# Letting the first scores of the last layer in a few products later

## The chip, the cores and the metric

The kernel runs on one core of a Trainium2 chip, in one launch. The metric is the device time of that launch in microseconds, taken as the median of several runs. TensorE multiplies matrices, VectorE and ScalarE do elementwise work and reductions, GpSimd does a little arithmetic and issues some loads, and SyncE issues most of the loads.

## The reference

Two layers act on 256 latent tokens (`x`) and 256 context tokens (`ctx`) of width 2048. Each layer has one wide input projection whose columns are shared out among three branches: a gated MLP that mixes positions, windowed attention with grouped queries, and a Fourier mix. The branches are gated, joined and projected back. The change touches the attention of the second layer, where only the latent tokens ask:

```
def window_attention(q, k, v, k_ctx, v_ctx, sink):
    ...
    s_loc = jnp.einsum('bnqkgd,bnjkd->bnkgqj', qb, kw).astype(jnp.float32) * scale
    s_ctx = jnp.einsum('bnqkgd,bmkd->bnkgqm', qb, k_ctx).astype(jnp.float32) * scale
    ...
    s_loc = jnp.where(mask[None, :, None, None], s_loc, NEG_INF)
    sk = sink_column(sink, (bsz, nb, B_KV_HEADS, B_GROUP, CHUNK))
    n_ctx = k_ctx.shape[1]
    p = jax.nn.softmax(jnp.concatenate([sk, s_ctx, s_loc], axis=-1), axis=-1)
    p_ctx = p[..., 1:1 + n_ctx].astype(v.dtype)
    p_loc = p[..., 1 + n_ctx:].astype(v.dtype)
    o = (jnp.einsum('bnkgqm,bmkd->bnqkgd', p_ctx, v_ctx)
         + jnp.einsum('bnkgqj,bnjkd->bnqkgd', p_loc, vw))
    return o.reshape(bsz, s, B_WIDTH)
```

There are 8 query heads of width 128 and 2 key/value heads. Queries and keys of the latent tokens are rotated (`rope_2d`) first.

## The kernel before, in words

Every large product is done in split precision. A weight tile `raw` of 128x1024 is loaded, ScalarE rounds it to a high part `whi` (L458) and VectorE subtracts to get the low part `wlo` (L460). Activations are split in the same way into pairs (`split_into`, L507 on ScalarE and L508 on VectorE).

TensorE's instruction order is written out by hand. In layer 1 a unit of 128 projected columns (`tunit1`) is 8 products of 512 columns (L627) on the first weight tile, 8 of 256 columns with its low part (L629), 8 of 256 with the second tile's low part, and 8 of 512 on the second tile. There are 8 such units for the queries (phase `q1`), one per head, and then 8 for the gate of the attention (phase `bg1`). When a unit is done, `joined` adds its two halves (L612 on ScalarE, L613 on VectorE).

The attention of a head is a generator, `attention(h, ps)`, that runs beside the units behind its own. Its pieces are these:

- the rotation of the query (`rope`: four copies L932 on ScalarE, L934 to L936 on VectorE) and its split (L507, L508);
- the scores: six products of 512 columns (L490 to L492) into two tiles `sc`, one per half of the queries; then the mask (L954), the row maximum (L956), the exponentials (L969, L976), the sum (L979), its reciprocal (L980) and the scaling of the probabilities (L985);
- twice, a group of four transposes (L1005) whose result is copied to a split pair (L507 of 512 columns on ScalarE, L508 on VectorE), and behind each such pair six products with the values into `o` (L490 to L492), one step later.

Between the pieces the generator yields a delay. A small clock, `Later`, holds them: each product of a unit moves it on by what the product is reckoned to take (`PASS`), and a piece whose delay has passed is emitted there, in TensorE's order, between two products of a unit. The delays are `YQ` from the rotation to the scores, `YA` from the scores to the first transposes, and `YB` from one group of transposes to the next:

```
    YQ, YA, YB = [5.5, 6.8], [10.0, 8.6], [3.8, 4.0]
```

A delay counts from where the piece before was really emitted. ScalarE's, VectorE's and SyncE's orders are not written by hand in this part: a scheduler sorts their instructions by priority, dependences and its own reckoning of times, and the engines then keep to that order.

Beside all this VectorE multiplies the modulation weights of the last gate, two instructions per loaded tile `mraw` (L290), placed among the other work as its priority allows.

Of the kernel before, what the change touches and what calls it, by code (L numbers as in the profile page):

```python
# [66 lines left out]
def trunk_kernel(ctx: ExitStack, tc: tile.TileContext, xT, xhalf, cT, wss, wsl, wmod, win, wout0, wout1, const, vec, rows,  # L67
# [9 lines left out]
    def sb(shape, dt, tag, bufs=1):  # L77
        cnt[0] += 1
        return pool.tile(shape, dt, tag=tag, bufs=bufs, name=f"{tag}_{cnt[0]}")

    def w2k(shape, dt=F32):
        return sb(shape, dt, "w2k", W2K)

    def mm_ps(name="mm"):
        cnt[0] += 1
        return psum.tile([P, 512], F32, tag="mm", bufs=6, name=f"ps_{name}_{cnt[0]}")

    def ms_ps(name="ms"):
        cnt[0] += 1
        return psum.tile([P, 512], F32, tag="ms", bufs=2, name=f"ps_{name}_{cnt[0]}")  # L90
# [251 lines left out]
    NX, AHEADX, LATE = 4, 2, 12  # L342
    YX, YC, YE = [2.4, 1.4, 1.8], 1.5, 5.0
    YQ, YA, YB = [5.5, 6.8], [10.0, 8.6], [3.8, 4.0]

    def pace():

        state["owed"] += RATE.get(state["phase"], 0.0) / 2
        while state["owed"] >= 1:
            state["owed"] -= 1  # L350
            with low(LAG), tc.issue_after(W.last.ins):
                next(mods, None)
# [136 lines left out]
    def mm3(ps, st, mv, start, stop):  # L489
        PE.matmul(ps, st[0], mv[0], start=start, stop=False)  # L490
        PE.matmul(ps, st[0], mv[1], start=False, stop=False)  # L491
        PE.matmul(ps, st[1], mv[0], start=False, stop=stop)  # L492

    def part(w, c):

        def of(t):
            if not isinstance(t, list):
                return t[:, c]
            n = t[0].shape[-1]
            return t[c.start // n][:, c.start % n:c.start % n + c.stop - c.start]  # L500

        return of(w[0]), of(w[1])
# [3 lines left out]
    def split_into(hi, lo, src):  # L506
        A.copy(hi, src)  # L507
        V.tensor_tensor(out=lo, in0=src, in1=hi.bitcast(F32), op=ALU.subtract)  # L508
        return hi, lo
# [134 lines left out]
    def layer(l):  # L644
        last = l == 1
# [278 lines left out]
        def rope(hi, lo, ps, ctx=None):  # L924

            if ctx is None and hi.shape[-1] > S:
                ctx = ps[:, S:T]
            nrot[0] += 1
            rot = rots[nrot[0] % 4]
            for a in range(4):  # L930
                b = a ^ 1
                A.copy(rot[32 * a:32 * a + 32], ps[32 * b:32 * b + 32, 0:S])  # L932
            t = w2k([P, S])
            V.tensor_tensor(out=t, in0=ps[:, 0:S], in1=cc("cos"), op=ALU.mult)  # L934
            V.tensor_tensor(out=rot, in0=rot, in1=cc("sin"), op=ALU.mult)
            V.tensor_tensor(out=rot, in0=rot, in1=t, op=ALU.add)  # L936
            split_into(hi[:, LAT], lo[:, LAT], rot)
            if hi.shape[-1] > S:
                split_into(hi[:, CTX], lo[:, CTX], ctx)
# [4 lines left out]
        def attention(h, ps):  # L944
            g = h // 4
            q = w2k([P, n], F32R), w2k([P, n], F32R)
            rope(*q, ps)
            yield YQ[l]
            sc, mx = [], sb([P, 4], F32, "mx", 2)
            for b in range(2):  # L950
                s = mm_ps("sc")
                mm3(s, part(q, slice(b * P, (b + 1) * P)), kt[g], True, True)
                edge = s[:, (1 - b) * P:(2 - b) * P]
                V.tensor_tensor(out=edge, in0=edge, in1=split["m0"][:, b], op=ALU.add)  # L954
                sc.append((s, T))
                V.tensor_reduce(out=mx[:, b:b + 1], in_=s, axis=mybir.AxisListType.X, op=ALU.max)  # L956
            if not last:
                s = mm_ps("scc")
                for b in range(2):
                    mm3(s[:, b * S:(b + 1) * S], part(q, slice(S + b * P, S + (b + 1) * P)),  # L960
                        part(kt[g], CTX), True, True)
                sc.append((s, S))
                V.tensor_reduce(out=mx[:, 2:4], in_=s.rearrange("p (b k) -> p b k", k=S),
                                axis=mybir.AxisListType.X, op=ALU.max)
            nm = sb([P, 4], F32, "nm", 2)
            V.tensor_scalar(out=nm[:, :nt], in0=mx[:, :nt], scalar1=-SCALE, scalar2=nskb[:, h:h + 1],
                            op0=ALU.mult, op1=ALU.min)
            es = sb([P, 4], F32, "es", 2)
            A.activation(es[:, :nt], nm[:, :nt], AF.Exp, bias=skb[:, h:h + 1])  # L969
            den = sb([P, 4], F32, "den", 2)  # L970
            prob = []
            for i, (s, w) in enumerate(sc):
                p = w2k([P, T])
                for b in range(T // w):
                    c = i + b
                    A.activation(p[:, b * w:(b + 1) * w], s[:, b * w:(b + 1) * w], AF.Exp, scale=SCALE,  # L976
                                 bias=nm[:, c:c + 1], accum_out=den[:, c:c + 1])
                prob.append(p)
            V.tensor_tensor(out=den[:, :nt], in0=den[:, :nt], in1=es[:, :nt], op=ALU.add)  # L979
            V.reciprocal(den[:, :nt], den[:, :nt])  # L980
            for i, (s, w) in enumerate(sc):
                for b in range(T // w):
                    c = i + b
                    with low(LOWP[l]):
                        A.activation(prob[i][:, b * w:(b + 1) * w], prob[i][:, b * w:(b + 1) * w], AF.Copy,  # L985
                                     scale=den[:, c:c + 1])
            yield YA[l]
            o, pts = None, []

            def pv(half):  # L990
                for j in range(2):
                    kk = 2 * half + j
                    dst, kv = (o[:, LAT], kk) if half < 2 else (o[:, CTX], 2 + j)
                    mm3(dst, part(vv, slice(kv * 256 + g * P, kv * 256 + (g + 1) * P)),
                        part(pts[half], slice(j * S, (j + 1) * S)), kk in (0, 4), kk in (3, 5))

            halves = 2 if last else 3
            for half in range(halves):
                tp = ms_ps("tp")
                for j in range(2):  # L1000
                    for b in range(2):
                        kk = 2 * half + j
                        src = prob[b][:, kk * P:(kk + 1) * P] if half < 2 else \
                            prob[2][:, b * S + j * P:b * S + (j + 1) * P]
                        PE.transpose(tp[:, (2 * j + b) * P:(2 * j + b + 1) * P], src, ident)  # L1005
                pts.append(split_into(w2k([P, 512], F32R), w2k([P, 512], F32R), tp))
                if half == 0:
                    o = mm_ps("o")
                else:
                    pv(half - 1)  # L1010
                yield YB[l]
            pv(halves - 1)
            A.copy(ysl(4 + h), o[:, 0:n])
# [57 lines left out]
        for h in range(8):  # L1071
            ps = tunit1([0])[0] if last else tunit(n)
            later.add(attention(h, ps))
            later.tick(0.0)
# [385 lines left out]
```

## Time and profile before

| what | value |
|---|---|
| median of three runs | 1130.13 us (1129.95 to 1130.45) |
| profiled execution, its time | 1130.9 us |
| profiled execution, its span | 1129.1 us |
| TensorE busy | 1118.5 us, 99% of the span |
| VectorE busy | 928.0 us, 82% |
| ScalarE busy | 526.0 us, 47% |
| mean granted TensorE clock | 0.999 |

The profile is of one execution. Its span runs from the first to the last instruction; the time of the run has 1.8 us more around it. In the timeline, each row has the start in us, the duration, the engine, the line of the kernel, the operation, what it writes and reads, and how many equal instructions were merged; a bracket tells how long the engine had been idle before it and whose work ended that.

### The profile page before, as it was taken

The page shows a single profiled execution, that of the slowest core. Times are in us where ns is not written, and L with a number is a line of the kernel's source. Part 1 is how long each engine was busy: PE and PEld are TensorE (multiplying, and loading weights), DVE is VectorE, ACT ScalarE, POOL GpSimd, SP SyncE. Part 2 cuts the span into 40 slices and gives each one's busy share as a digit, 9 for nine tenths or more (in the row PEclk, how much of TensorE's full clock was granted, in tenths as well). Part 3 has the DMA queues.
Part 4 walks back from the last instruction along what each step waited for, and adds up shares of the span by engine and source line. Part 5 has one row for each costly group of instructions (what it writes and reads, how often), then busy time and mean ns, then how long its engine had stood idle before and what let it go on. Part 6 is the DMA issues. An engine that isn't in the chain of part 4 may idle for free.

```text
span 1129.1 us, 16606 instructions
## 1 busy us (share of the span) xinstructions
PE 1118.5 (99%) x6108; PEld 920.4 (82%) x6108; DVE 928.0 (82%) x1633; ACT 526.0 (47%) x992; POOL 32.9 (3%) x43
## 2 busy tenths in 40 slices
PE   8999999999999999999999999999999999999998
PEld 3666788888888888888888888988888888888886
DVE  1578799989888897888999989396988788878874
ACT  5322533322234667632523334266665369867541
POOL 0000000000000000000000000030500000000000
PEclk9999999999999999999999999999999999999999
DMA  9999655566655344365566665385956785456972
GB/s 364 402 402 400 244 172 187 183 205 200 211 180 187 119 141 130 121 204 174 182 188 221 206 205 185 96 193 191 226 180 205 225 282 177 147 186 196 304 259 75
DMA packets 75138, 235.85 MB, mean 209 GB/s; under 512 B 8608, under 2 KB 13104, under 8 KB 75056
## 3 DMA queue, kind: packets, MB, share of 16 engines
q1 hardware_dynamic: 70272, 229.79, 60.8%
q0 software_dynamic: 4064, 3.69, 2.2%
q10 hardware_dynamic: 720, 1.31, 0.3%
q8 instruction: 48, 0.79, 0.3%
q14 instruction: 34, 0.28, 0.1%
HBM read 232.65 MB, written 2.10 MB: 208 GB/s over the span
## 4 chain that ended last, share of the span: by engine, by line
PE 94%; DMA 3%; ACT 1%; DVE 1%; issue 0%; ACTq 0%; POOLq 0%; DVEq 0%
PE ps_t L490 15%; PE ps_t L491 15%; PE ps_t L492 15%; PE ps_t L627 10%; PE ps_t L629 5%; PE ps_v L1065 3%; PE ps_y L490 3%; PE ps_y L492 3%; PE ps_y L491 3%; PE ps_av L490 2%; PE ps_mod L182 2%; PE ps_av L491 2%; PE ps_av L492 2%; PE ps_tp L1005 2%; PE ps_v L1067 1%; PE ps_au L490 1%
## 5 line engine op out<-in xcount | busy, mean ns | idle before, releaser
L458 ACT CAST whi<-raw 128x1024 fp32r<-128x1024 f32 (+1 forms) x209 | 216.2, 1037 | 292.5 <-PE ps_t L491 217.0
L460 DVE TENSOR_TENSOR wlo<-raw,whi 128x1024 fp32r<-128x1024 f32 (+1 forms) x209 | 251.0, 1205 | 50.4 <-ACT whi L458 43.8
L490 PE MATMUL ps_t<-hh,whi 128*128 128x512 f32 (+1 forms) x752 | 290.7, 387 | 0.0
L491 PE MATMUL ps_t<-hl,whi 128*128 128x512 f32 (+1 forms) x752 | 289.6, 385 | 0.0
L492 PE MATMUL ps_t<-hh,wlo 128*128 128x512 f32 (+1 forms) x752 | 289.4, 385 | 0.0
L252 DVE SCALAR_TENSOR_TENSOR macc<-mraw,cs,macc 128x512 f32<-128x512 f32 x360 | 251.0, 747 | 13.3 <-DMA mraw<-in_wmod_dram 12.8
L492 PEld LDWEIGHTS ps_t<-hh,wlo 128*128 128x128 f32 x752 | 141.3, 188 | 28.7
L490 PEld LDWEIGHTS ps_t<-hh,whi 128*128 128x128 f32 x752 | 141.3, 188 | 26.8
L491 PEld LDWEIGHTS ps_t<-hl,whi 128*128 128x128 f32 x752 | 141.4, 188 | 26.2
L627 PE MATMUL ps_t<-hh,whi 128*128 128x512 f32 x512 | 132.7, 394 | 0.0
L627 PEld LDWEIGHTS ps_t<-hh,whi 128*128 128x128 f32 x512 | 92.6, 188 | 16.8
L629 PE MATMUL ps_t<-hh,wlo 128*128 128x256 f32 x512 | 72.5, 282 | 0.0
L629 PEld LDWEIGHTS ps_t<-hh,wlo 128*128 128x128 f32 x512 | 68.5, 190 | 2.4
L572 ACT ACTIVATE hh<-w2k,sh 128x256 fp32r<-128x256 f32 x48 | 22.0, 502 | 73.5 <-DVE w2k L568 73.5
L490 PE MATMUL ps_y<-whi,hh 128*128 128x512 f32 x104 | 41.3, 397 | 0.0
L492 PE MATMUL ps_y<-whi,hh 128*128 128x512 f32 x104 | 40.6, 390 | 0.0
L491 PE MATMUL ps_y<-wlo,hh 128*128 128x512 f32 x104 | 40.5, 389 | 0.0
L490 PE MATMUL ps_av<-whi,hh 128*128 128x512 f32 x94 | 39.0, 415 | 0.6 <-ACT hh L572 0.6
L491 PE MATMUL ps_av<-wlo,hh 128*128 128x512 f32 x94 | 37.0, 394 | 0.0
L507 ACT CAST w2k<-ps_tp 128x512 fp32r<-128x512 f32 x40 | 23.4, 585 | 20.8 <-PE ps_scc L491 13.7
L508 DVE TENSOR_TENSOR w2k<-ps_tp,w2k 128x512 fp32r<-128x512 f32 x40 | 27.5, 688 | 4.7 <-ACT w2k L507 2.2
L612 ACT COPY join<-ps_t 128x256 f32<-128x256 f32 x34 | 12.4, 370 | 39.0 <-PE ps_t L627 38.9
(460 smaller groups left out, 1736.8 us busy)
## 6 DMA issues: line engine op xcount, KB each, us to landing
raw<-in_win_dram SPq DMA_DIRECT2D x160, 512.0 KB, 4.2
mraw<-in_wmod_dram SPq DMA_DIRECT2D x128, 512.0 KB, 4.3
raw<-in_wout_dram SPq DMA_DIRECT2D x60, 512.0 KB, 4.3
mraw<-in_wsl_dram SPq DMA_DIRECT2D x14, 512.0 KB, 7.1
yo<-in_wsl_dram SPq DMA_DIRECT2D x16, 256.0 KB, 7.2
macc<-in_wsl_dram SPq DMA_DIRECT2D x7, 512.0 KB, 7.7
vv<-in_wsl_dram SPq DMA_DIRECT2D x7, 512.0 KB, 8.3
mg<-in_wsl_dram SPq DMA_DIRECT2D x7, 512.0 KB, 9.0
```

Source lines behind the costliest of these rows:

```text
L182: PE.matmul(self.ps[32 * kk:32 * kk + 32, 0:self.N], cpad[:, kg * 4 + kk], self.w[kg * 4 + kk], start=kg == 0, stop=kg == 3, tile_position ...
L252: V.scalar_tensor_tensor(out=acc[:, s], in0=w[:, kk % 2], scalar=c, in1=acc[:, s], op0=ALU.mult, op1=ALU.add)
L458: A.copy(ph, rc)
L460: self.last = V.tensor_tensor(out=pl, in0=rc, in1=ph.bitcast(F32), op=ALU.subtract)
L490: PE.matmul(ps, st[0], mv[0], start=start, stop=False)
L491: PE.matmul(ps, st[0], mv[1], start=False, stop=False)
L492: PE.matmul(ps, st[1], mv[0], start=False, stop=stop)
L507: A.copy(hi, src)
L508: V.tensor_tensor(out=lo, in0=src, in1=hi.bitcast(F32), op=ALU.subtract)
L627: PE.matmul(ps, wk, h, start=k == 0, stop=k == KT - 1)
L629: PE.matmul(ps[:, 0:S], wk, h[:, 0:S], start=False, stop=False)
L1065: PE.matmul(vps[t], hs[t][0], wk, start=k == 0, stop=k == KT - 1)
```

## The change

The delay between the rotation of a query and its scores is made longer by 1.0 for one head, the first of the last layer. The pieces behind the scores take their delays from there.

```
     YX, YC, YE = [2.4, 1.4, 1.8], 1.5, 5.0
     YQ, YA, YB = [5.5, 6.8], [10.0, 8.6], [3.8, 4.0]
+    YFIRST = 1.0
...
             q = w2k([P, n], F32R), w2k([P, n], F32R)
             rope(*q, ps)
-            yield YQ[l]
+            yield YQ[l] + (YFIRST if last and h == 0 else 0.0)
             sc, mx = [], sb([P, 4], F32, "mx", 2)
```

More of the change, by code (lines that the diff above doesn't have):

```diff
@@ L344, in trunk_kernel @@
     YQ, YA, YB = [5.5, 6.8], [10.0, 8.6], [3.8, 4.0]
+    YFIRST = 1.0
     def pace():
@@ L947, in attention @@
             rope(*q, ps)
-            yield YQ[l]
+            yield YQ[l] + (YFIRST if last and h == 0 else 0.0)
             sc, mx = [], sb([P, 4], F32, "mx", 2)
```

## The prediction

> **What bounds the kernel now.** I read the page's first part, then its chain of work, then the timeline of TensorE, VectorE and ScalarE around the first heads of layer 1.
>
> ```profile
> PE 1118.5 (99%) x6108; PEld 920.4 (82%) x6108; DVE 928.0 (82%) x1633; ACT 526.0 (47%) x992; POOL 32.9 (3%) x43
> ...
> PE 94%; DMA 3%; ACT 1%; DVE 1%; issue 0%; ACTq 0%; POOLq 0%; DVEq 0%
> ```
>
> TensorE is the bound: it is busy 99% of the span and carries 94% of the chain. Its list of instructions is written by hand and keeps all of them here, so the change can only alter how long TensorE stands still. The time is TensorE's work plus its holes, and I count the holes.
>
> The edited step lies at 919 us. Call the eight projections of layer 1's q columns Q0 to Q7. Each is 8 products of 512 columns, 16 of 256 (low weights), 8 of 512. TensorE from the start of Q2 on:
>
> ```profile
> 915.22 3.82 PE L627 MATMUL ps_t<-hh,whi 128*128 128x512 f32 x16
> 919.12 0.50 PE L490 MATMUL ps_sc<-kt,w2k 128*128 128x512 f32 x1
> ...
> 920.41 0.50 PE L492 MATMUL ps_sc<-kt,w2k 128*128 128x512 f32 x1 [0.56 <-DVE w2k L508]
> ...
> 921.44 2.06 PE L629 MATMUL ps_t<-hh,wlo 128*128 128x256 f32 x16
> 923.34 3.82 PE L627 MATMUL ps_t<-hh,whi 128*128 128x512 f32 x16
> 926.99 0.39 PE L490 MATMUL ps_sc<-kt,w2k 128*128 128x512 f32 x1
> ...
> 928.38 2.07 PE L629 MATMUL ps_t<-hh,wlo 128*128 128x256 f32 x16
> 930.29 2.00 PE L627 MATMUL ps_t<-hh,whi 128*128 128x512 f32 x8
> 933.07 0.33 PE L1005 MATMUL ps_tp<-identr,w2k 128*128 128x128 f32 x1 [0.78 <-ACT w2k L985]
> 933.68 0.55 PE L1005 MATMUL ps_tp<-identr,w2k 128*128 128x128 f32 x3 [0.29 <-ACT w2k L985]
> 933.99 2.09 PE L627 MATMUL ps_t<-hh,whi 128*128 128x512 f32 x8
> ...
> 942.21 0.60 PE L1005 MATMUL ps_tp<-identr,w2k 128*128 128x128 f32 x4
> 942.57 2.09 PE L627 MATMUL ps_t<-hh,whi 128*128 128x512 f32 x8
> ...
> 947.82 0.39 PE L491 MATMUL ps_o<-w2k,vv 128*128 128x256 f32 x1 [0.22 <-DVE w2k L508]
> ...
> 952.39 2.10 PE L627 MATMUL ps_t<-hh,whi 128*128 128x512 f32 x8
> ...
> 961.67 2.11 PE L627 MATMUL ps_t<-hh,whi 128*128 128x512 f32 x8
> ```
>
> Steps from these rows: a 512-column product 0.228 us ((926.99-923.34)/16), a 256-column one 0.119 ((930.29-928.38)/16), six score products 1.39 (928.38-926.99), four transposes 0.36 (942.57-942.21).
>
> Three holes before. The scores of head 0: TensorE is free at 915.22+3.65=918.87 and goes on with Q2 at 921.44; less 1.39 that is 1.18 lost, waiting for q's low part. The first transposes: free at 930.29+1.82=932.11, going on at 933.99; less 0.36 that is 1.52 lost, waiting for ScalarE's scaling of the probabilities (L985). Unit Q5: 9.82 (942.57 to 952.39) against 9.28 for Q6 with the same content (952.39 to 961.67), so 0.54 lost. In all 3.2 us.
>
> **The change part by part.** The two programs' queues, laid side by side, show this. No instruction is added or dropped. On TensorE head 0's six scores move behind nine low-weight products of Q2. Its first transposes move five products later, from ahead of Q4 to behind Q4's fifth product; its second transposes and first P·V, both inside Q4's last eight before, now stand behind Q4, directly ahead of head 1's transposes; its second P·V moves seven products later in Q5. GpSimd's queue is the same. On SyncE some 512 KB loads swap places. ScalarE and VectorE are ordered by a scheduler, and both are re-sorted from here to the end of the attention. The swap that matters, on ScalarE:
>
> ```
> between scaling head 0 (L985 x2) and copying its first transposed block (L507)
> before: q copy L507, L969, L976 x2
> after:  q copy L507, L969, join L612, weights L458, L976 x2, L932 x3, L985 x2,
>         L932, weights L458, L969, join L612, q copy L507, weights L458
> ```
>
> *The scores.* The rows of VectorE that they need:
>
> ```profile
> 912.78 1.23 DVE L460 TENSOR_TENSOR wlo<-raw,whi 128x1024 fp32r<-128x1024 f32 x1 [0.49 <-ACT whi L458]
> ...
> 919.94 0.42 DVE L508 TENSOR_TENSOR w2k<-mgl,w2k 128x256 fp32r<-128x256 f32 x1
> ```
>
> They now begin at 918.87+9x0.119=919.94. The third product, the first to read q's low part, comes at 919.94+0.46=920.40; that part is written at 920.36. The ninth low-weight product needs the second weight tile, written at 914.0. So the 1.18 go (bounds: all of it, or 0.1 less). Q2 ends at 919.94+1.39+0.83+1.82=923.98, before at 923.34+1.82=925.16.
>
> *The first transposes.* ScalarE's rows:
>
> ```profile
> 925.38 0.37 ACT L612 COPY join<-ps_t 128x256 f32<-128x256 f32 x1 [3.16 <-PE ps_t L627]
> ...
> 929.67 1.65 ACT L932 COPY mgl<-join 32x256 f32<-32x256 f32 x4
> 931.34 1.05 ACT L458 CAST whi<-raw 128x1024 fp32r<-128x1024 f32 x1
> 932.30 1.33 ACT L985 ACTIVATE w2k<-w2k,den 128x512 f32<-128x512 f32 x2
> 933.53 0.39 ACT L507 CAST w2k<-mgl 128x256 fp32r<-128x256 f32 x1
> 933.83 0.30 ACT L969 ACTIVATE es<-nm,skb 128x2 f32<-128x2 f32 x1
> 934.03 0.67 ACT L976 ACTIVATE w2k<-ps_sc,nm 128x512 f32<-128x512 f32 x1
> ...
> 935.35 0.57 ACT L507 CAST w2k<-ps_tp 128x512 fp32r<-128x512 f32 x1
> 935.94 1.34 ACT L985 ACTIVATE w2k<-w2k,den 128x512 f32<-128x512 f32 x2
> 937.19 0.35 ACT L612 COPY join<-ps_t 128x256 f32<-128x256 f32 x1
> 937.44 2.00 ACT L458 CAST whi<-raw 128x1024 fp32r<-128x1024 f32 x2
> ```
>
> The join starts 0.22 after Q2's end and the scaling 6.92 after the join (932.30-925.38). The same work stands between them now, with one rope copy (L932) moved ahead, which waits for VectorE's join for at most 0.2. So the join starts at 924.2 and the scaling at 931.2, 1.1 earlier. TensorE reaches the transposes at 923.98+1.82+1.39+1.91+1.82+1.14=932.06. Before, the second one began at 933.68, 0.76 after the second scaling (932.92); now at 931.82+0.76=932.58. The next product came 0.31 later; now 932.89. Lost: 932.89-932.06-0.36=0.47 where 1.52 were. So far 2.2 us are won.
>
> *The first P·V.* TensorE goes on with 3 products, 1.39 of scores, 1.91, 1.82, and is through Q4 at 938.69 and through the second transposes at 939.05. P·V needs the copy of the first transposed block, which followed 3.05 behind the scaling (935.35-932.30). Now, by the list above, from 931.2: scaling 1.23, L507 0.30, L969 0.20, L612 0.25, L458 0.96, L976 1.32 (935.35-934.03), three L932 1.25, scaling 1.25, L932 0.42, L458 0.96, L969 0.20, L612 0.25, L507 0.30, L458 0.96: the copy starts at 941.05 and ends at 941.62. Each of these finds its input: the joins wait for Q3 and Q4, over at 930.9 and 938.7, and stand at 932.9 and 939.5. The low part of the block is VectorE's, queued behind the low part of the last weight tile, which waits for L458:
>
> ```profile
> 937.76 0.68 DVE L508 TENSOR_TENSOR w2k<-ps_tp,w2k 128x512 fp32r<-128x512 f32 x1
> ...
> 938.69 1.22 DVE L460 TENSOR_TENSOR wlo<-raw,whi 128x1024 fp32r<-128x1024 f32 x1
> ```
>
> That is 941.14+1.22+0.68, about 943.1. Before, this low part was written at 938.44, ahead of need. So the first P·V product starts at 941.65 rather than 939.05 and the second at 943.1: a new hole of 2.6+1.3=3.9. Behind it stand the other five products and head 1's transposes: Q5 starts at 943.1+0.60+0.36=944.06, before 942.57. TensorE is 1.5 late. Bounds: none of the hole if the copies were early (TensorE would be 2.4 ahead), and 4.5 if a queue entry waits for another 0.6; I take the walked value, since every entry has its own row.
>
> *Behind it.* ScalarE and VectorE have run on during the hole. Q5's second P·V stands seven products later and its copies were started some 5 us ahead, so Q5 should take the 9.28 of Q6: 0.54 come back. Nearest to being late is head 1's first P·V, whose low copy I find within 0.1 of its need. The swapped loads are covered:
>
> ```profile
> raw<-in_win_dram SPq DMA_DIRECT2D x160, 512.0 KB, 4.2
> mraw<-in_wmod_dram SPq DMA_DIRECT2D x128, 512.0 KB, 4.3
> ```
>
> The modulation tile that lets a weight tile pass ahead of it is issued when its buffer comes free, at about 927.5, and read at about 937; the weight tile is read by the L458 at 938.4. Landing takes 4.3; without that cover ScalarE's queue, and so the hole, would be longer by what is missing.
>
> Sum: -1.18-1.05+3.9 on the holes comes to +1.67; the direct difference at Q5 is +1.5, which I take; less 0.54 is +1.0 us. The profiled execution has a span of 1129.1 and a time of 1130.9; its span would become 1130.1 and its time 1131.9. The three runs' median is 1130.13, 0.8 below that run, so I forecast 1131.1. The bounds of the hole and the last digit of each step make it 1130.4 to 1131.9.
>
> **The rivals.** *The hole cools TensorE's clock* (slower). The clock at the end of the kernel, in stretches of one us (granted clock third from the right):
>
> ```profile
> 1127.00:1128.00 1.00, 0.00 (x0) 0.00 (x0) 0.00 (x0) 0.00 (x0) 0.00 (x0) 0.78 0.51 186
> 1128.00:1129.10 1.10, 0.00 (x0) 0.00 (x0) 0.00 (x0) 0.00 (x0) 0.00 (x0) 0.50 0.00 0
> ```
>
> With the 0.78 of the first stretch the clock fell to half at about 1127.56, and the last product of the kernel ends at 1124.59:
>
> ```profile
> 1123.46 1.13 PE L1207 MATMUL ps_x<-yo,w2k 128*128 128x256 f32 x4 [0.46 <-ACT w2k L1199]
> ```
>
> So 3.0 us of rest were enough there. The new hole is 2.6 us, one product of 0.12, and 1.3 us. If that one product doesn't count, the clock is halved when TensorE resumes; if it stays so for another 3.0 us, 1.5 us of work are lost, and the time is 1131.1+1.5=1132.6. It decides if the pair of holes counts as one of over 3.0. Against it: neither hole alone is as long, and the holes of before (up to 1.5) left the clock at full. [...]
>
> *The copies are not late* (faster). If ScalarE and VectorE got the first block ready by 939.05, the holes shrink by 1.18+1.05+0.54 and the time is 1127.4. It needs ScalarE 2.6 us ahead of my walk, against a queue of fourteen entries without a wait in it; hardly likely. Half of it, the scores' 1.18 alone kept, gives 1129.0.
>
> *The queue is later still* (slower). If head 1's first P·V misses its copies too, by about the 1.2 of a low weight tile in the way, the time is 1132.3. Its 0.1 of slack speaks for it; that the tile ahead of it is ready early, against.
>
> **How the numbers follow.** My forecast gets 0.62, the cooled clock 0.17, the later queue 0.09, the scores' gain alone 0.05, the copies in time 0.07. A difference of 0.2%, 2.26 us, is about what a measurement of this kernel tells from none: faster means below 1127.87, slower above 1132.39. The first holds the last case, 0.06 of its 0.07. The second holds most of the cooled clock and some of the later queue, 0.16. The rest is 0.78. The range leaves out both faster cases and the upper third of the cooled ones, 0.18: 1129.6 to 1132.8.
>
> **What would show it.** Right: no wait of the scores of head 0; the first transposes' wait under 0.6; a wait of the first P·V of head 0 at about 941.6 and 943.1, for ScalarE's and VectorE's L507 and L508; Q5 9.3 long; granted clock 1.00 from 943 on. Wrong: P·V without a wait, or ScalarE's copy of head 0's first block before 940; a clock below 1.00 behind the hole; Q5 over 9.6.

## The result and the profile after

| | before | after |
|---|---|---|
| median | 1130.24 us (7 runs) | 1133.57 us (7 runs, 1133.45 to 1134.4) |
| profiled execution, its time | 1130.9 us | 1133.84 us |
| profiled execution, its span | 1129.1 us | 1132.1 us |
| mean granted TensorE clock of each run | 0.999 or 1.000 | 0.998 or 0.997 |

The ratio is 1.003, with a 95% interval from 1.0019 to 1.0042. The kernel became slower by 3.3 us, where 1.0 was forecast. All line numbers behind the added one are one higher than before: the split is now L508 and L509, the transposes L1006, the units L628 and L630. In the experiments with more added lines they are higher by so much again.

TensorE's timeline of the changed kernel, from the end of Q1 to Q7 (start, duration, engine, line, what is written and read, how many):

```profile
914.69 3.82 PE L628 MATMUL ps_t<-hh,whi 128*128 128x512 f32 x16
...
919.41 0.40 PE L491 MATMUL ps_sc<-kt,w2k 128*128 128x512 f32 x1
...
931.66 0.96 PE L1006 MATMUL ps_tp<-identr,w2k 128*128 128x128 f32 x4
932.38 0.94 PE L628 MATMUL ps_t<-hh,whi 128*128 128x512 f32 x3
...
938.29 0.60 PE L1006 MATMUL ps_tp<-identr,w2k 128*128 128x128 f32 x4
941.40 0.38 PE L491 MATMUL ps_o<-w2k,vv 128*128 128x256 f32 x1 [2.51 <-ACT w2k L508]
942.87 0.39 PE L492 MATMUL ps_o<-w2k,vv 128*128 128x256 f32 x1 [1.08 <-DVE w2k L509]
...
943.57 1.00 PE L1006 MATMUL ps_tp<-identr,w2k 128*128 128x128 f32 x4
944.23 3.39 PE L628 MATMUL ps_t<-hh,whi 128*128 128x512 f32 x8
947.46 0.39 PE L491 MATMUL ps_sc<-kt,w2k 128*128 128x512 f32 x1
...
952.50 0.37 PE L491 MATMUL ps_o<-w2k,vv 128*128 128x256 f32 x1
953.04 0.38 PE L492 MATMUL ps_o<-w2k,vv 128*128 128x256 f32 x1 [0.17 <-DVE w2k L509]
...
955.24 2.10 PE L628 MATMUL ps_t<-hh,whi 128*128 128x512 f32 x8
...
964.53 0.71 PE L628 MATMUL ps_t<-hh,whi 128*128 128x512 f32 x2
```

The scores of head 0 wait no more. The two brackets at 941.40 and 942.87 are the new hole: first ScalarE's copy of head 0's first transposed block is missing, then VectorE's low part of it. Behind them eight ordinary products take 3.23 us (944.23 to 947.46). ScalarE and VectorE at the same place, the scaling of head 0 first:

```profile
930.69 1.33 ACT L986 ACTIVATE w2k<-w2k,den 128x512 f32<-128x512 f32 x2
...
940.76 0.58 ACT L508 CAST w2k<-ps_tp 128x512 fp32r<-128x512 f32 x1
```

```profile
941.00 1.22 DVE L461 TENSOR_TENSOR wlo<-raw,whi 128x1024 fp32r<-128x1024 f32 x1
942.13 0.68 DVE L509 TENSOR_TENSOR w2k<-ps_tp,w2k 128x512 fp32r<-128x512 f32 x1
```

The windows of one us each (the granted clock is third from the right) tell why the products behind the hole are slow:

```profile
943.00:944.00 1.00, 1.00 (x8) 1.00 (x9) 0.95 (x2) 0.98 (x4) 0.00 (x0) 0.81 1.09 197
944.00:945.00 1.00, 1.00 (x5) 0.90 (x4) 0.96 (x4) 0.96 (x3) 0.00 (x0) 0.50 0.45 143
945.00:946.00 1.00, 1.00 (x4) 0.79 (x3) 0.79 (x2) 0.12 (x1) 0.00 (x0) 0.50 0.88 340
946.00:947.00 1.00, 1.00 (x4) 0.72 (x3) 0.00 (x0) 1.00 (x2) 0.00 (x0) 0.50 0.75 205
947.00:948.00 1.00, 1.00 (x6) 0.82 (x5) 0.00 (x0) 0.56 (x2) 0.00 (x0) 0.98 0.88 324
```

0.81 in one us means 0.38 us at half rate, 0.98 means 0.04: TensorE ran at half clock from 943.62 to 947.04, for 3.42 us; windows of 0.01 us put the two ends at 943.621 and 947.034, 3.413 us apart.

Q1's last row starts at 914.69 where before had 915.22, so this trace runs 0.53 earlier; with 0.53 added its times stand beside the prediction's:

| step | before | forecast | measured |
|---|---|---|---|
| scores of head 0 begin | 918.87 free, held up | 919.94 | 919.94 |
| product behind the first transposes | 933.99 | 932.89 | 932.91 |
| second transposes done | | 939.05 | 938.65 + 0.53 = 939.18 |
| first P·V product | no wait | 941.65 | 941.93 |
| second P·V product | no wait | 943.1 | 943.40 |
| Q5 starts | 942.57 | 944.06 | 944.76 |
| Q5 lasts | 9.82 | 9.28 | 11.01 |
| Q6 starts | 952.39 | 953.34 | 955.77 |

Q6 then lasts 9.29 (955.24 to 964.53), as the 9.28 of before. So everything is decided by the start of Q6, 3.38 us later than before, and the forecast missed 2.43 of it: 0.3 at the second P·V product, 2.1 between it and the start of Q6.

### The profile page after: what moved, and what is told of

Same layout as the page of the kernel before. It is cut to its first block, busy times and chain, and to the rows that moved or that the text cites. A ratio compares the mean times of both kernels' runs of the same rounds, so it can differ in the third digit from the quotient of the medians.

```text
span 1132.1 us, 16609 instructions
## 1 busy us (share of the span) xinstructions
PE 1119.5 (99%) x6105; PEld 921.7 (81%) x6108; DVE 928.4 (82%) x1633; ACT 526.6 (47%) x992; POOL 32.8 (3%) x43
## 3 DMA queue, kind: packets, MB, share of 16 engines
q10 hardware_dynamic: 720, 1.31, 0.3%
## 4 chain that ended last, share of the span: by engine, by line
PE 96%; DVE 2%; ACT 1%; DMA 1%; issue 0%; POOLq 0%; DVEq 0%; ACTq 0%
PE ps_t L491 15%; PE ps_t L492 15%; PE ps_t L493 15%; PE ps_t L628 10%; PE ps_t L630 5%; PE ps_v L1066 3%; PE ps_y L491 3%; PE ps_y L493 3%; PE ps_y L492 3%; PE ps_mod L182 2%; PE ps_av L491 2%; PE ps_av L492 2%; PE ps_av L493 2%; PE ps_tp L1006 1%; PE ps_v L1068 1%; PE ps_au L491 1%
## 5 line engine op out<-in xcount | busy, mean ns | idle before, releaser
L459 ACT CAST whi<-raw 128x1024 fp32r<-128x1024 f32 (+1 forms) x209 | 216.1, 1038 | 290.3 <-PE ps_t L492 216.4
L628 PE MATMUL ps_t<-hh,whi 128*128 128x512 f32 x512 | 133.8, 397 | 0.0
L628 PEld LDWEIGHTS ps_t<-hh,whi 128*128 128x128 f32 x512 | 93.7, 190 | 17.2
L630 PE MATMUL ps_t<-hh,wlo 128*128 128x256 f32 x512 | 72.5, 282 | 0.0
L630 PEld LDWEIGHTS ps_t<-hh,wlo 128*128 128x128 f32 x512 | 68.6, 190 | 2.5
L508 ACT CAST w2k<-ps_tp 128x512 fp32r<-128x512 f32 x40 | 23.4, 585 | 21.6 <-PE ps_scc L492 13.7
L509 DVE TENSOR_TENSOR w2k<-ps_tp,w2k 128x512 fp32r<-128x512 f32 x40 | 27.4, 685 | 3.4 <-ACT w2k L508 2.0
L986 ACT ACTIVATE w2k<-w2k,den 128x512 f32<-128x512 f32 (+1 forms) x48 | 28.2, 647 | 1.1 <-DVE den L981 0.9
```

The lines of the kernel that those rows point to most:

```text
L459: A.copy(ph, rc)
L628: PE.matmul(ps, wk, h, start=k == 0, stop=k == KT - 1)
L630: PE.matmul(ps[:, 0:S], wk, h[:, 0:S], start=False, stop=False)
```

## The experiments

The theory (A) from this profile: the walk of the queues was right; the missing 2.4 us are mostly the cooled clock, which the prediction had as a rival, and the hole that cools it comes from the new place of one copy in ScalarE's list. The rival (B): the hole and the waits behind it cost the 3.3 us by themselves, and the moved scores or the moved P·V are the cause. All medians together:

| kernel | median | ratio to before, 95% interval | runs with a mean clock of 0.998 or less |
|---|---|---|---|
| after | 1133.57 | 1.0019 to 1.0042 | 7 of 7 |
| fill9 | 1132.35 | 1.0012 to 1.0031 | 3 of 10 |
| fill4 | 1133.41 | 1.0021 to 1.0038 | 7 of 11 |
| fill_second | 1133.62 | 1.0014 to 1.0034 | 6 of 9 |
| fill_both | 1132.15 | 1.0005 to 1.0023 | 0 of 11 |
| steps_alone | 1133.86 | 1.0023 to 1.0048 | 5 of 5 |
| scores_alone | 1129.46 | 0.9986 to 1.0003 | 0 of 11 |
| transposes_back | 1130.35 | 0.999 to 1.0008 | 0 of 11 |
| one_product | 1135.44 | 1.0032 to 1.0057 | 5 of 5 |
| scores_075 | 1129.39 | 0.9983 to 1.0 | 0 of 11 |

The kernel before ran beside each group, at 1130.12 to 1130.25, never below a mean clock of 0.999.

### Is it the clock? Work put into the holes

**fill9.** In `attention`, behind the last transposes of head 0 and ahead of `pv`:

```
+                    if last and h == 0:
+                        for _ in range(FILL):          # 9
+                            PE.matmul(o, kt[0][0][:, 0:P], kt[0][0], start=True, stop=True)
                     pv(half - 1)
```

> The changed kernel with nine products of 512 columns (0.228 us each, 2.05 in all) written ahead of head 0's first P·V, whose own first product overwrites what they leave. They stand in the 2.51 us in which TensorE waits there, so they cost nothing and only keep it at work. Theory A (the pair of holes halves the granted clock, which costs Q5 about 1.6 us): no stretch below 1.00 behind the holes, Q5's first eight products in 1.9 us instead of 3.2, and the time about 1.65 below the changed kernel's 1133.6: 1131.9. Rival B (the holes and the wait behind them cost the 3.3 us by themselves; the low clock only goes with them): 1133.6, as the changed kernel.

Seven of the ten runs had a mean clock of 0.999 or 1.000 and took 1131.88 to 1133.02; the 1133.02 is the profiled one, which was 0.7 late already at the scores of head 0 (920.09 in its trace, 919.41 in that of after). The other three had 0.998 and took 1133.60 to 1133.71. Where the clock holds, the time is the 1131.9 of theory A or a little more, without the P·V products coming any earlier. That it falls at all, with 0.4 and 1.1 us of bracketed rest left, was expected by neither theory.

**fill4.** The same with `FILL = 4`.

> As the one with nine, but four such products: 0.91 us of the first hole are filled, 1.6 us of it stay, then one product, then the 1.1 us of the second hole: 2.7 us together. If the two holes count as one and it takes about 3.0 us of rest (the prediction's number), the clock stays at 1.00 and the time is 1131.9, as with nine. If a shorter rest is enough, the clock falls as in the changed kernel: 1133.6. With the holes taken one by one (1.6 and 1.1) it would stay too; but then it should not have fallen in the changed kernel either, whose longest single hole is 2.5.

Neither: four runs at 1131.92 to 1132.44 with a full clock, seven at 1133.37 to 1135.92 with 0.998 or 0.997. The same program has both outcomes, so in these eleven runs no fixed length of the rest, single or summed, decided. The author's reading, an estimate from this and from the 3.413 us of after: the clock followed the rest within stretches of about that length, which began at a chance moment of the kernel. Four of the seven, at 1134.49 and above, lie higher than one such fall explains; no trace of them was kept.

The traces agree with such stretches. The end of the kernel after, and the end of the profiled run of fill4, which did not fall before:

```profile
1131.00:1132.00 1.00, 0.00 (x0) 0.00 (x0) 0.00 (x0) 0.00 (x0) 0.00 (x0) 0.68 0.00 0
```

```profile
1128.00:1129.00 1.00, 0.00 (x0) 0.00 (x0) 0.00 (x0) 0.00 (x0) 0.00 (x0) 0.85 0.54 201
```

In after the clock is back at 947.04 and falls again at 1131.36, 184.32 us later; a 54th part of it is 3.413, the time at half rate in the same trace (a 53rd would be 3.478, a 55th 3.351). The traces of steps_alone, fill_second and one_product have the same 184.32 between these two moments. On the estimate from these two numbers that one stretch of 3.413 us followed the other without a gap, they can be counted back from the fall at the end. In after the count lands on 943.63, the fall behind the hole. In fill4, from 1128.70, it lands on 940.97, inside the rest: 1.76 us of rest lie in the stretch ahead of that moment, 1.45 in the next, and the clock stayed. In fill9's profiled run, which did not fall either, the parts are 1.67 and 0.40.

**fill_both.** Nine products as above, and into the second hole:

```
+                    for _ in range(FILL2 if last and h == 0 and kk == 0 else 0):   # 8
+                        PE.matmul(dst, st[0], mv[0], start=True, stop=True)
                     mm3(dst, st, mv, kk in (0, 4), kk in (3, 5))
```

> The changed kernel with both holes filled: nine products of 512 columns ahead of head 0's first P·V (2.05 us) and that P·V's first product of 256 columns written eight times more (8 x 0.119 = 0.95 us, each time from the start) before the one that counts. The holes keep their ends, which ScalarE and VectorE set. Theory A (the clock falls when TensorE stood still for too large a part of one stretch of 3.4 us, wherever that stretch happens to begin; nine products alone left enough rest for 3 of 10 runs at a mean clock of 0.998 and 1133.6): no run below 0.999, all of them near 1132.1, the time of the undisturbed ones with nine. Rival B (the slow ones have another cause): again some at 1133.6.

All eleven runs lie between 1131.98 and 1132.44, clock 0.999 or 1.000. TensorE's timeline of this kernel:

```profile
938.53 2.33 PE L1017 MATMUL ps_o<-kt 128*128 128x512 f32 x9
941.29 1.21 PE L999 MATMUL ps_o<-w2k,vv 128*128 128x256 f32 x8 [0.42 <-ACT w2k L509]
942.34 0.28 PE L492 MATMUL ps_o<-w2k,vv 128*128 128x256 f32 x1
942.76 0.39 PE L493 MATMUL ps_o<-w2k,vv 128*128 128x256 f32 x1
...
943.82 2.10 PE L629 MATMUL ps_t<-hh,whi 128*128 128x512 f32 x8
945.76 0.40 PE L492 MATMUL ps_sc<-kt,w2k 128*128 128x512 f32 x1
```

The P·V still begins where ScalarE lets it, and its second counting product (942.76) comes where VectorE lets it; of TensorE's 4.1 us of rest 1.0 is left, and the eight products of Q5 take 1.94 us (943.82 to 945.76) in place of 3.23. So the clock's share is 1133.57 - 1132.15 = 1.42 us, and 1.9 of the 3.3 stay for the hole and what follows it.

**fill_second.** `FILL = 0`, the second hole filled as above.

> The changed kernel with the second hole alone filled (the P·V's first product written eight times more, 0.95 us of the 1.08); the first hole of 2.51 us stays whole. Theory A (a stretch of 3.4 us that is idle for more than about half halves the clock for the next one, and the stretches begin anywhere): a hole of 2.5 us lies for 1.7 us or more in one stretch in (3.4+2.5-2x1.7)/3.4 = 0.73 of the runs, so about 7 of 10 runs near 1133.5 with a mean clock of 0.998 or less and the others near 1132.1. Rival B (the prediction's: the two holes count as one of over 3.0 us, and neither alone is enough): all runs near 1132.1 at 0.999 or 1.000.

Six of nine fell (1133.12 to 1134.12), three did not (1131.64 to 1132.05): theory A, whose 3.4 us is the time at half rate in after (3.42) and steps_alone (3.40), and whose "more than about half" is the author's estimate. One hole of 2.5 us was enough in these six. The windows of the profiled run, one of those that fell:

```profile
942.00:943.00 1.00, 1.00 (x8) 0.87 (x6) 0.99 (x2) 0.98 (x3) 0.00 (x0) 0.71 0.71 254
...
945.00:946.00 1.00, 1.00 (x5) 0.87 (x4) 0.99 (x4) 0.56 (x2) 0.00 (x0) 0.58 0.75 287
```

Half rate from 942.42 to 945.84, 3.42 us again, and it sets in while TensorE works, 0.85 us behind the end of the hole:

```profile
941.57 1.38 PE L999 MATMUL ps_o<-w2k,vv 128*128 128x256 f32 x8 [2.50 <-ACT w2k L509]
```

Of the 3.41 us before the fall 2.56 are rest (939.01 to 941.57), not right ahead of it.

### Where does the hole come from?

**scores_alone.** The delay behind the scores gives back what the one ahead of them got:

```
-            yield YA[l]
+            yield YA[l] - (YFIRST if last and h == 0 else 0.0)
```

> Head 0's scores get the 1.0 of delay, and the delay behind them is shortened by 1.0, so that its transposes and P·V stand where they stood before the change. On ScalarE the copy of the first transposed block then stands five or six entries behind the scaling, not fourteen. Theory A (the loss comes from the later steps alone, since they send the copy behind fourteen entries): no hole at the first P·V, clock at 1.00, the scores' 1.18 us won: about 1129.0. Rival B (moving the scores alone already makes the copies late, since the exponentials and all that follows start from them): a wait at the first P·V and 1131 or more.

No wait at the first P·V, clock full, 1129.46: theory A, though 0.5 short of 1129.0. ScalarE's copy starts 4.3 us behind the scaling (3.05 in before), not 10.1 as in after:

```profile
930.40 1.33 ACT L986 ACTIVATE w2k<-w2k,den 128x512 f32<-128x512 f32 x2
...
934.67 0.58 ACT L508 CAST w2k<-ps_tp 128x512 fp32r<-128x512 f32 x1
```

The trace runs 0.82 earlier than before's (scores at 919.12, 919.94 in the walk); with that, Q6 starts 1.6 earlier than before (949.94 + 0.82 against 952.39). About 1.0 of it is given back in the third unit of the gate. In the traces' own times the unit's first eight products start 2.59 us earlier than before (987.07 against 989.66), the next unit's only 1.62 (995.93 against 997.55). On ScalarE the copy of head 5's second block now stands behind one more weight tile (L459), which in before comes later; VectorE, also behind one more weight tile, is free at the same moment, and the low part follows the copy:

```profile
987.19 1.05 ACT L459 CAST whi<-raw 128x1024 fp32r<-128x1024 f32 x1
...
989.66 0.59 ACT L508 CAST w2k<-ps_tp 128x512 fp32r<-128x512 f32 x1
```

```profile
990.28 0.69 DVE L509 TENSOR_TENSOR w2k<-ps_tp,w2k 128x512 fp32r<-128x512 f32 x1
```

```profile
991.02 0.39 PE L492 MATMUL ps_o<-w2k,vv 128*128 128x256 f32 x1 [0.31 <-DVE w2k L509]
```

**steps_alone.** The other half: `YQ` as before, and `yield YA[l] + (YFIRST if last and h == 0 else 0.0)`.

> The other half: head 0's scores stay where they were, and the delay behind them is 1.0 longer, so that its transposes and P·V stand where the change puts them. ScalarE's copy of the first block again stands behind some fourteen entries. Theory A (the later steps make the loss): the 1.18 us of the scores' wait stay, the hole at the first P·V is there with about 2.6 and 1.3 us, the clock falls to half behind it: before + 4.0, about 1134.2. Rival B (the loss comes from the scores' move): no hole, about 1130 or a little less, by what the first transposes' wait shrinks.

1133.86, and both waits, 2.38 and 0.34 long, with half rate from 943.26 to 946.66 (the rows, and the first and the last window of it):

```profile
942.12 0.39 PE L491 MATMUL ps_o<-w2k,vv 128*128 128x256 f32 x1 [2.38 <-ACT w2k L508]
942.85 0.39 PE L492 MATMUL ps_o<-w2k,vv 128*128 128x256 f32 x1 [0.34 <-DVE w2k L509]
```

```profile
943.00:944.00 1.00, 1.00 (x7) 1.00 (x8) 1.00 (x2) 0.98 (x3) 0.00 (x0) 0.63 0.79 315
...
946.00:947.00 1.00, 1.00 (x5) 0.79 (x4) 0.83 (x2) 1.00 (x2) 0.00 (x0) 0.67 0.99 401
```

The later steps make the loss; the second wait is shorter than the 1.3 expected. Together with scores_alone this divides the change: its one half wins 0.7, its other half loses 3.7.

**transposes_back.** After, with the first transposes alone at their old place:

```
-            yield YA[l]
+            yield YA[l] - (YFIRST if last and h == 0 else 0.0)
...
-                yield YB[l]
+                yield YB[l] + (YLATER if last and h == 0 and half == 0 else 0.0)   # 1.0
```

> The changed kernel with head 0's first transposes alone put back ahead of Q4's first product; the scores and all P·V products stand where the change has them, behind Q4 and directly ahead of head 1's transposes. ScalarE's copy of the first transposed block is then sorted right behind one scaling, q's copy and the exponentials, not behind fourteen entries. Theory A (the hole comes from the place of that copy in ScalarE's list, and this place from where the transposes stand): no wait of the first P·V, clock at 1.00, the scores' 1.18 us kept: 1129.0 to 1129.6. Rival B (the P·V's new place, five products later and stacked on head 1's transposes, makes the loss): 1131 or more.

The hole is gone, with the P·V standing exactly where after has it. ScalarE's copy follows 4.3 us behind the scaling, and the first P·V product comes without a wait:

```profile
930.62 1.33 ACT L987 ACTIVATE w2k<-w2k,den 128x512 f32<-128x512 f32 x2
...
934.89 0.58 ACT L509 CAST w2k<-ps_tp 128x512 fp32r<-128x512 f32 x1
```

```profile
939.75 0.36 PE L492 MATMUL ps_o<-w2k,vv 128*128 128x256 f32 x1
...
949.55 0.39 PE L493 MATMUL ps_o<-w2k,vv 128*128 128x256 f32 x1 [1.31 <-DVE w2k L510]
```

But the time is 1130.35, not 1129.0 to 1129.6: the last row is head 1's P·V, which waits for a low part that VectorE does behind a weight tile,

```profile
947.67 1.22 DVE L462 TENSOR_TENSOR wlo<-raw,whi 128x1024 fp32r<-128x1024 f32 x1
948.81 0.68 DVE L510 TENSOR_TENSOR w2k<-ps_tp,w2k 128x512 fp32r<-128x512 f32 x1
```

which is the prediction's rival of the later queue, at about its price (1.31 for 1.2) and in another kernel. Of the expectation the hole's cause is borne out, the time is not.

**one_product.** Scores as before, `YA` longer by 0.1 for head 0, so that its first transposes move one product.

> The scores stay where they were before the change, and the delay behind them is 0.1 longer: head 0's first transposes move one product (0.23 us) later, into Q4, and what hangs on them by one. On ScalarE the copy of the first block already falls back by eleven entries, as in the changed kernel. Theory A (the place in ScalarE's list is what counts, not how far TensorE's step moved): from the scaling's 932.30 in the trace of before the copy starts about 8.7 later, at 941.0, and ends at 941.5; TensorE is at the first P·V at 940.2, so 1.4 us of hole there and 0.6 to 1.3 more for the low part; less the 0.54 of Q5 the time is 1.5 to 2.2 above before: 1131.7 to 1132.4, and up to 1.5 more in runs where the clock falls. Rival B (one product moved costs what one product is worth, or nothing): 1130.0 to 1130.5.

ScalarE's copy stands 9.3 us behind the scaling, so one product of 0.23 us sends it back as the change does:

```profile
931.57 1.33 ACT L986 ACTIVATE w2k<-w2k,den 128x512 f32<-128x512 f32 x2
...
940.83 0.56 ACT L508 CAST w2k<-ps_tp 128x512 fp32r<-128x512 f32 x1
```

The hole is there, and the clock falls inside it (the windows behind the rows):

```profile
939.18 0.60 PE L1006 MATMUL ps_tp<-identr,w2k 128*128 128x128 f32 x4
941.45 0.38 PE L491 MATMUL ps_o<-w2k,vv 128*128 128x256 f32 x1 [1.67 <-ACT w2k L508]
943.13 0.58 PE L492 MATMUL ps_o<-w2k,vv 128*128 128x256 f32 x1 [1.30 <-DVE w2k L509]
```

```profile
942.00:943.00 1.00, 0.00 (x0) 0.00 (x0) 1.00 (x2) 0.07 (x1) 0.00 (x0) 0.58 0.55 74
...
948.00:949.00 1.00, 1.00 (x3) 0.77 (x3) 0.77 (x1) 0.96 (x3) 0.00 (x0) 0.51 0.03 8
```

Half rate lasts from 942.16 to 948.98, 6.8 us. That is the 1135.44, far over the 1131.7 to 1132.4: theory A names the right mechanism, and the expectation had the hole too short (3.5 us from 939.54 to 943.13 less one product, not 2.0 to 2.7) and one stretch at half rate where there were two.

**scores_075.** As scores_alone, with `YFIRST = 0.75`.

> Only head 0's scores move, by 0.75 in place of 1.0, which puts them behind six of Q2's low-weight products in place of nine; the delay behind them is shortened by as much. ScalarE's and VectorE's lists then stay all but those of before. Theory A (scores moved alone keep their gain as long as the two lists aren't re-sorted): they start at 919.58, the third product has to wait from 920.04 to 920.41, so 0.4 of the 1.18 us stay and 0.8 are won; nothing of it is given back later: 1129.4, at or under the 1129.46 of the scores moved alone by 1.0, which wins 1.9 by Q6 and gives about 1 back behind head 7. Rival B (the later loss comes with any earlier TensorE): 1129.8 to 1130.2.

1129.39, 0.86 under before, with every one of eleven runs (1129.32 to 1129.78) below every run of before beside it (1130.02 to 1131.38): theory A. The scores still wait a little,

```profile
919.69 0.51 PE L493 MATMUL ps_sc<-kt,w2k 128*128 128x512 f32 x1 [0.20 <-DVE w2k L509]
```

and nothing is given back: in the traces' own times the third unit of the gate starts 1.42 us earlier than before (988.24 against 989.66), and so does the next (996.13 against 997.55). (The "head 7" of the expectation is head 5.) Its median is the lowest here, 0.08% under before, though the interval just reaches 1.0; from scores_alone, 0.07 us above it, it can't be told apart.

## Why the prediction was wrong

**The walk of the queues: right.** Scores without a wait, the first transposes' next product at 932.91 for 932.89, ScalarE's copy of the first block at 940.76 + 0.53 = 941.29 for 941.05, the first P·V at 941.93 for 941.65 and the second at 943.40 for 943.1. The hole was forecast at 2.6 + 1.3 and is 2.75 + 1.35 (938.65 to 941.40, one product of 0.12, to 942.87). This term was 0.3 too small: ScalarE's copy starts 0.24 later than walked, behind a scaling that is on time (930.69 + 0.53 = 931.22 for 931.2).

**The clock: the step that failed.** The forecast took a granted clock of 1.00 from 943 on, and gave the cooled clock 0.17. It happened in all seven runs. The working had its number and weighed it wrongly: it read the 3.0 us between the kernel's last product and the clock's fall as the length that an unbroken rest must have, and set against it that "neither hole alone is as long". In fill_second one hole of 2.5 us was enough in 6 of 9 runs, fill4 (7 of 11) and fill9 (3 of 10) show that the same program fell in some runs and not in others, and in after and fill_second the clock fell when TensorE had resumed, 0.75 and 0.85 us behind the end of the hole. Nor is the 3.0 a fixed length at the kernel's end: in scores_alone the clock falls there 1.94 us behind the last product (1123.00 to 1124.94), in scores_075 4.04 us (1123.18 to 1127.22). What fits all runs is an estimate from them, not a measurement: that the rest within a stretch of 3.413 us, the time at half rate in after, decided here. The profiled falls inside the kernel had 2.5 to 2.9 us of rest in the 3.41 us ahead of them. Of a pair of holes of 4.1 us in all, one such stretch holds at least half, 2.05 us, wherever the stretches begin; the clock fell in 7 of 7 runs of after. The price was right: 1.5 forecast, 1.42 by the medians of after and fill_both, 1.59 by the trace (head 1's transposes 0.66 for 0.36, Q5's eight products 3.23 for 1.94), and 1.5 and 1.7 between the medians of the runs that fell and those that did not, in fill9 and in fill_second.

**Behind it: half right.** "Q5 should take the 9.28 of Q6" failed, apart from the clock, at the place that was named as nearest to being late: head 1's first P·V waits from 952.70 (one step of 0.20 behind 952.50, as that step is where nothing waits) to 953.04, 0.34 us. The rival of the later queue, priced at 1.2, thus came at a quarter of its size; transposes_back shows it in full.

**The sum.** Of the 2.43 us by which Q6 is later than forecast, 0.3 are the hole, 0.1 the five products behind it, 0.30 the transposes and 1.29 the products at half rate, 0.34 head 1's P·V, and 0.1 is not accounted for. The forecast's case without the clock would have been 1132.15, fill_both, not 1131.1; of this 1.05 the terms above name 0.74.

**Cause and direction.** That the swap on ScalarE matters, not the scores, was right: scores_alone and steps_alone divide it so, and transposes_back removes the hole by moving the copy forward with the P·V left where it is. The size of the move on TensorE is not what counts: one_product moves the transposes by one product and makes the larger loss. Why the scheduler sends the copy back for it wasn't tried.

## What to carry to other kernels

Where a hand-written engine order meets sorted ones, cost a move by the new place of every instruction that hangs on it in the other queues: here a step that goes 0.23 us later on TensorE sends a copy 5 us or more back on ScalarE. When a walk ends in a hole of TensorE, set its rest beside what was measured here: with holes of 4.1 us in all and one product of 0.12 us between them (after) the clock fell to half in 7 of 7 runs, with 2.06 (fill9) in 3 of 10, with 1.0 (fill_both) in none of 11. So the half clock, 1.4 to 1.7 us here, belongs in the forecast itself, as a share of the runs. Filling the holes with products that are overwritten bought back the 1.42 us of the clock in fill_both, and not the 1.9 us of the hole and what follows it.

## What the chip showed that was not expected

The half rate lasts 3.42 us in after, 3.40 in steps_alone, 3.42 in fill_second (read from shares of two digits) and 6.82, twice the 3.413 that narrower windows give in after, in one_product. In the 3.41 us ahead of each fall TensorE was not idle: counted by the steps of its rows it rested 2.55 us in after (1.20 ahead of the lone product at 941.40, 1.35 behind it), 2.56 in fill_second and 2.5 in one_product, three quarters of the stretch, and 2.9 in steps_alone. Fill9's rests, at most 0.70 and 1.36, sum to 2.06 and went with a fall in 3 of 10 runs; those of fill_both, 1.0, in none of 11; the 1.52 of before's first transposes in none of its runs. The most that a stretch held without a fall, counted back as above, is the 1.76 of fill4's profiled run. These counts stand for these runs alone: where the three falls of fill9 lay is not recorded, and what amount of rest brings a fall was not measured.

In one_product the first 3.41 us at half rate, 942.16 to 945.57, still hold 0.97 us of the hole (to 943.13), and the clock stayed at half for as long again; in after and fill_second, where TensorE worked throughout, it came back after 3.42 us. In this one trace a hole that went on when the clock fell went with twice the time at half rate; whether it was the cause was not tried.
